# Attention values made token-major by transposing DMAs of 16-bit halves instead of float32 transposes on TensorE

## The chip, the cores and the metric

The kernel runs on one core of a Trainium2 chip. The metric is the device time of one execution in microseconds, as a median over runs; lower is better. The engines are named as the profile names them: PE is TensorE, DVE is VectorE, ACT is ScalarE, POOL is GpSimd, SP is SyncE, which issues most DMAs.

## The reference

Two layers work on 272 tokens (16 meta tokens and a sequence of 256) with 1024 features in float32. In each layer a mixer has three branches, and a convolutional feed-forward block follows:

```
proj = rms_norm(h) @ w_in          # rq rk rv rg  hq hf hi hg  dq dk dv  gates
o_ret = retention(rq, rk, rv, rg)  # 4 heads, values 256 wide
o_hg  = hgrn2(hq, hf, hi, hg)      # 8 heads, values 128 wide
o_da  = diff_attention(dq, dk, dv) # 8 heads, values 128 wide
y = sum(sigmoid(gates) * (branches @ w_branch))
h = h + y @ w_out
h = h + (silu(gate) * val) @ w_ffn_out   # gate, val: a convolution over tokens of rms_norm(h) @ w_ffn_in
```

The values of the three branches are rv, hi and dv. Each branch multiplies a matrix of weights between tokens by its values, so that the sum runs over tokens.

## The kernel before, in words

**Layout.** Features lie on the 128 partitions and tokens along the free dimension (T = 272). Each matrix product with a weight is three matmuls that take float32 apart into a rounded high part and a rest: `wh·xh`, `wh·xl`, `wl·xh` (L917 to L919, in `products`). One weight tile is 128 x 128, and one call of `products` makes two output tiles of 128 features (f = 0, 1), side by side in two PSUM banks (tag "main", two pairs of banks).

**Weights.** `_Weights` (L600) loads the weights in chunks of eight tiles, 128 x 1024 float32, by one DMA each on SP's queue (L628) into `wraw` (three buffers). ACT copies a chunk to `whi` (rounded), DVE subtracts to get `wlo`; both have four buffers. There are 404 chunks.

**Order.** The kernel does not issue instructions as its code runs. Each call through `_Engine` (L558) records an operation in `_Plan` with an engine, an assumed cost, a key (the time at which it is due), and the tiles that it reads and writes (`add`, L379, with overlaps found by `_span`, L370). `order` (L438) then simulates the five engines with these costs: an engine takes the operation that can start first, by key where several can, and `start` (L466) gives none before its buffers are free. What comes out is the fixed instruction order of every engine. The products have keys that follow each other on a clock; everything else is planned around them. `key += 2.0` moves what follows to a later due time. A sequence `ORDER` lists the products and, by marks, where the attention work of a branch begins to be spread between them and by when it has to be done.

**Values.** The matmuls of the attention need values with tokens on partitions, while `products` leaves features on partitions. `values` (L1491) lets ACT copy the two output tiles, 128 x 2 x 272, from PSUM to `vsrc` in SBUF (`evacuate`, L929). `to_tokens` (L953) then has PE transpose four blocks of 128 x 128 against an identity matrix into a PSUM bank (tag "bank", tile `vt`): two feature tiles by two blocks of 128 tokens. ACT copies the bank in two instructions of 128 x 256 to the token-major tile (`rvt`, or `vt` for hi and dv). The 16 tokens left over are gathered from `vsrc` by POOL into a tile `tails`, which `tail_tokens` (L962) transposes on PE once for each group of heads. In the loop over `ORDER` (L1555) the calls stand under `name == "rv"` (L1611) and `name in ("hi", "dv")` (L1620). rv, hi and dv have four calls each in a layer: 24 in all. In the order of work hi 0 and 1 come first, then hi 2, hi 3 and rv 0 to 3 in a row, then dv 0 and 1, and dv 2 and 3.

**Norms.** `mean` (L972) and `head_rsqrt` (L987) sum over partitions; both use a temporary tile "hso" for sums, and `head_rsqrt` lets POOL's all-reduce write it before ACT takes the logarithm and the exponential into `r`.

Of the kernel before, what the change touches and what calls it, by code (L numbers as in the profile page):

```python
# [11 lines left out]
F32 = mybir.dt.float32  # L12
F32R = mybir.dt.float32r
U8 = mybir.dt.uint8
AF = mybir.ActivationFunctionType
ALU = mybir.AluOpType
PSUM = bass.MemoryType.PSUM
# [2 lines left out]
P = 128  # L20
# [3 lines left out]
T = META + SEQ  # L24
# [13 lines left out]
TAIL = T - 2 * P  # L38
# [296 lines left out]
class _Plan:  # L335
# [34 lines left out]
    def _span(self, ap):  # L370
        step = ap.ap[0][0]
        lo = ap.offset % step
        hi = lo + 1 + sum((n - 1) * abs(s) for s, n in ap.ap[1:])
        if ap.tensor.name in self.psum:

            lo, hi = lo // BANK * BANK, -(-hi // BANK) * BANK
        return ap.tensor.name, lo, hi
# [60 lines left out]
    def order(self):  # L438

        times, mains = [m.key for m in self.main], set(self.main)  # L440
        for op in self.ops:
            i = bisect.bisect_right(times, op.key - EARLY) - 1
            if i >= 0 and op not in mains:
                self.queue(op, self.main[i])
        left = {}
        for op in self.ops:
            for n in op.tiles:
                left[n] = left.get(n, 0) + 1
        free = {tag: [0.0] * k for tag, k in self.room.items()}
        held, out = set(), []  # L450
        engines = {"pe": 0.0, "act": 0.0, "dve": 0.0, "pool": 0.0, "sp": 0.0}
        later = {e: [] for e in engines}
        now = {e: [] for e in engines}
        count = 0
        tables = "le"

        def push(op):
            nonlocal count
            count += 1
            heapq.heappush(later[op.engine], (op.ready, count, op))  # L460

        for op in self.ops:
            if op.need == 0:
                push(op)

        def start(op, t):  # L466

            want = {}
            for n in op.tiles:
                if n not in held:  # L470
                    want[self.tag[n]] = want.get(self.tag[n], 0) + 1
            for tag, k in want.items():
                if len(free[tag]) < k:
                    return None
                t = max(t, sorted(free[tag])[k - 1])
            return t

        def rank(op):
            late = 8.0 if op.func in self.SETS and self.SETS[op.func] != tables else 0.0
            return op.key + late  # L480

        self.end = engines
        self.busy = {e: 0.0 for e in engines}
        taken = 0.0

        def comes(op):
            return op.count < self.MANY or (int(taken) - self.BEGIN.start) % self.PIECE < len(self.BEGIN)

        todo = len(self.ops)
        while len(out) < todo:  # L490
            best = None
            for e, t0 in engines.items():
                while later[e] and later[e][0][0] <= t0:
                    _, c, op = heapq.heappop(later[e])
                    now[e].append((c, op))
                found = None
                for c, op in now[e]:
                    t = start(op, t0) if comes(op) else None
                    if t is not None and (found is None or (t, rank(op), c) < found[:3]):
                        found = (t, rank(op), c, op)  # L500
                if later[e]:
                    t1 = later[e][0][0]
                    if found is None or t1 < found[0]:
                        found = (t1, 0.0, -1, None)
                if found is not None and (best is None or found[0] < best[0]):
                    best = found + (e,)
            if best is None:
                raise RuntimeError("no order: " + str([(e, [o.tiles for _, o in now[e]][:4]) for e in now]))
            t, _, c, op, e = best
            if op is None:  # L510
                engines[e] = t
                continue
            now[e].remove((c, op))
            cost = op.cost
            if e == "dve" and engines["pool"] > t:

                cost += min(engines["pool"] - t, self.SHARED * cost)
            if op.func in self.SETS and self.SETS[op.func] != tables:
                tables = self.SETS[op.func]
                cost += self.SWITCH  # L520
                if tables == "le":
                    out.append(None)
                    todo += 1
            for n in op.tiles:
                if n not in held:
                    held.add(n)
                    f = free[self.tag[n]]
                    f.remove(min(f))
            engines[e] = t + cost
            self.busy[e] += cost  # L530
            taken += op.count * (1 + self.SEMS)
            done = t + cost + (2.0 if e == "sp" else 0.0)
            for n in op.tiles:
                left[n] -= 1
                if left[n] == 0:
                    free[self.tag[n]].append(done + self.FREE)
            for o in op.after:
                o.need -= 1
                o.ready = max(o.ready, done + (self.CROSS if o.engine != e else 0.0))
                if o.need == 0:  # L540
                    push(o)
            if op.run is not None:
                out.append(op)
            else:
                todo -= 1
        return out
# [11 lines left out]
class _Engine:  # L558
# [5 lines left out]
    def __getattr__(self, method):  # L564
        f = getattr(self.engine, method)

        def call(*args, **kw):
# [13 lines left out]
            if method == "reciprocal":  # L581
                cost += 7 * self.each * n
            elif method == "tensor_tensor_scan":
                cost += self.each * n
            elif method == "transpose":
                cost = 0.11
            elif method == "matmul" and args[1].dtype == F32R:
                cost = max(0.107, n / 2400 + 0.003)
            elif method == "matmul":
                cost = max(0.214 if args[1].shape[-1] > 32 else 0.07, 4 * n / 2400)  # L590
            elif method == "dma_start":
                cost = self.fixed + self.each * n * outs[0].shape[0]

# [60 lines left out]
def _trace(ctx, tc, plan, a, depth, probe):  # L654
# [35 lines left out]
    def temp(cols, tag, bufs=2):  # L690
        return new(tp, [P, cols], F32, tag, bufs, tag)
# [4 lines left out]
    def bank(name):  # L696
        return new(bp, [P, 512], F32, "bank", 2, name)
# [252 lines left out]
        act.activation(hi, x, AF.Copy)  # L950
        tt(lo, x, hi.bitcast(F32), SUB)

    def to_tokens(src, vt, e):  # L953

        pt = bank("vt").rearrange("p (f c e) -> p f c e", f=2, c=2)
        for f in range(2):
            for c in range(2):
                pe.transpose(pt[:, f, c, :], src[:, f, c * P : (c + 1) * P], ident)
        for f in range(2):
            act.activation(vt[:, :, e + f * P : e + (f + 1) * P], pt[:, f], AF.Copy)  # L960

    def tail_tokens(tails):  # L962

# [8 lines left out]
    def mean(ones_, x):  # L972
# [1 line left out]

        n = x.shape[1]
        sums = x[top]
        other = temp(T, "hso")[top, :n]
        act.activation(other, x[low], AF.Copy)
        tt(sums, sums, other, ADD)
        both = new(tp, [P, T], F32R, "hsh", 1, "hsh")[:, :n]  # L980
# [6 lines left out]
    def head_rsqrt(r, x, func, scale=1.0):  # L987

        n = x.shape[1]
        sq = x  # L990
        if func != AF.Copy:
            sq = temp(T, "hsq")[:, :n]
            act.activation(sq, x, func)
        sums = temp(T, "hso")[:, :n]
        pool.partition_all_reduce(sums, sq, channels=P, reduce_op=bass.bass_isa.ReduceOp.add)
        rsqrt(r, sums, scale / P)

    def split_blocks(name, blocks, t0):

# [8 lines left out]
    for li in range(depth):  # L1008
# [479 lines left out]
                st[name] = slot4(name)  # L1488
            return st[name]

        def values(ps, vt, e):  # L1491

            src = temp2("vsrc")
            evacuate(src, ps)
            plan.key += 2.0
            to_tokens(src, vt, e)
            return src

        def final():

            turns.pop(0)
# [53 lines left out]
        for name, j in ORDER:  # L1555
# [31 lines left out]
            if name in BASE:  # L1587
# [23 lines left out]
                elif name == "rv":  # L1611
                    if j == 0:
                        st["rvt"] = [slot("rvt")[:, : 8 * P].rearrange("p (c e) -> p c e", c=2) for _ in range(2)]
                        st["tails"] = temp(P, "tails")
                    src = values(ps, st["rvt"][j // 2], (j % 2) * 2 * P)
                    tails = st["tails"].rearrange("p (e h t) -> p e h t", e=2, h=4)
                    pool.tensor_copy(tails[:, :, j, :], src[:, :, 2 * P :])
                    if j == 3:
                        st["rvs"] = tail_tokens(st["tails"])
                elif name in ("hi", "dv"):  # L1620
                    n = name[0] + "v"
                    b = j // 2
                    if j % 2 == 0:
                        st[f"{n}t{b}"] = slot("vt")[:, : 8 * P].rearrange("p (c e) -> p c e", c=2)
                        st["tails"] = temp(P, "tails")
                        if name == "hi":
                            pool.memset(st["tails"][:, 4 * TAIL :], 0.0)
                    src = values(ps, st[f"{n}t{b}"], (j % 2) * 2 * P)
                    tails = st["tails"].rearrange("p (g h t) -> p g h t", g=2, h=4)[:, :, two, :]
                    pool.tensor_copy(tails[:, 0], src[:, :, 2 * P :])  # L1630
                    if name == "dv":
                        pool.tensor_copy(tails[:, 1], src[:, :, P : P + TAIL])
                    if j % 2:
                        st[f"{n}s{b}"] = tail_tokens(st["tails"])
                else:
# [101 lines left out]
```

## Time and profile before

| | |
|---|---|
| median of three runs | 1294.4 us (1294.36 to 1294.51) |
| the profiled execution's own time | 1293.94 us |
| its span in the profile | 1292.2 us |
| mean granted TensorE clock | 0.998 of full speed |
| HBM read | 216.19 MB, 168 GB/s over the span |

The span reaches from the first to the last instruction of the profiled execution. In the rows of the profile an instruction is named by line, engine, operation and tiles (out<-in), followed by counts, busy time and mean duration. All operations that the planner records have one line, L595 before the change, so groups are told apart by their tiles. "PEld" is the loading of weights into TensorE, which overlaps the matmuls; "SPq" is the instruction stream of SP, which issues DMAs. A row of waits reads: who waited, for whom, microseconds in total, times, longest.

### The profile page before, as it was taken

How to read it: one execution, taken by the hardware profiler on the slowest of the kernel's cores; microseconds unless marked ns; L12 is line 12 of the kernel's file. 1: busy time of each engine (PE TensorE's matmuls, PEld its weight loads, DVE VectorE, ACT ScalarE, POOL GpSimd, SP SyncE). 2: the span in 40 equal slices, each digit the busy share in tenths (PEclk: the TensorE clock that was granted, in tenths of full speed). 3: DMA queues.
4: the chain of work that ended last, by engine and by line, in shares of the span. 5: the costliest groups of instructions: out<-in, count | busy, mean ns of one | idle time of the engine just before them, and what ended most of it. 6: DMA issues, size and time to landing. Idle time of an engine off the chain costs nothing.

```text
span 1292.2 us, 27078 instructions
## 1 busy us (share of the span) xinstructions
PE 1284.3 (99%) x10921; PEld 1263.7 (98%) x10921; DVE 975.6 (75%) x1657; ACT 827.8 (64%) x1404; POOL 174.3 (13%) x206
## 2 busy tenths in 40 slices
PE   9999999999999999999999999999999999999998
PEld 9999999999999999999999999999999999999986
DVE  7685887698585789886565867976986867898753
ACT  6765465756576568776456664657566765787743
POOL 5001101313122020000020011012132220200000
PEclk9999999999999999999999999999999999999999
DMA  8644554444545555555555455544445466556653
GB/s 277 200 155 157 166 177 131 136 151 147 175 133 178 180 163 181 179 180 168 176 178 182 162 165 178 172 140 140 159 144 180 131 195 197 163 190 201 199 187 106
DMA packets 60750, 218.99 MB, mean 169 GB/s; under 512 B 6865, under 2 KB 6993, under 8 KB 60625
## 3 DMA queue, kind: packets, MB, share of 16 engines
q1 hardware_dynamic: 60336, 216.74, 52.1%
q8 instruction: 86, 1.41, 0.5%
q10 hardware_dynamic: 288, 0.52, 0.1%
q14 instruction: 40, 0.32, 0.1%
HBM read 216.19 MB, written 1.05 MB: 168 GB/s over the span
## 4 chain that ended last, share of the span: by engine, by line
PE 98%; DMA 0%; SPq 0%; DVE 0%; issue 0%; ACT 0%; DVEq 0%
PE main L919 29%; PE main L917 29%; PE main L918 28%; PE fo L1533 2%; PE fo L1531 2%; PE fo L1532 2%; PE ds L1394 1%; PE do L595 1%; PE ro L595 1%; PE ho L595 1%; PE vt L595 1%; PE lev L1117 1%; PE wt L595 1%; DMA wraw<-in_w 0%; PE s L595 0%; PE px L595 0%
## 5 line engine op out<-in xcount | busy, mean ns | idle before, releaser
L917 PE MATMUL main<-xh,whi 128*128 128x272 f32 (+1 forms) x2368 | 688.3, 291 | 0.5 <-ACT whi L595 0.5
L919 PE MATMUL main<-xh,wlo 128*128 128x272 f32 (+1 forms) x2368 | 679.4, 287 | 0.5 <-DVE wlo L595 0.4
L918 PE MATMUL main<-xl,whi 128*128 128x272 f32 (+1 forms) x2368 | 670.2, 283 | 0.0
L595 DVE TENSOR_TENSOR wlo<-wraw,whi 128x1024 fp32r<-128x1024 f32 (+1 forms) x408 | 509.4, 1254 | 200.5 <-ACT whi L595 197.2
L595 ACT ACTIVATE whi<-wraw 128x1024 fp32r<-128x1024 f32 (+1 forms) x408 | 426.6, 1048 | 221.3 <-PE main L918 143.9
L918 PEld LDWEIGHTS main<-xl,whi 128*128 128x128 f32 x2368 | 449.2, 190 | 0.4
L917 PEld LDWEIGHTS main<-xh,whi 128*128 128x128 f32 x2368 | 445.3, 188 | 1.9 <-ACT whi L595 0.7
L919 PEld LDWEIGHTS main<-xh,wlo 128*128 128x128 f32 x2368 | 444.5, 188 | 1.2 <-DVE wlo L595 1.1
L595 POOL PARTITION_ALL_REDUCE hso<-hsq x36 | 74.5, 2091 | 94.8 <-ACT hsq L595 94.6
L595 POOL TENSOR_TENSOR y<-h,rstd 128x272 f32<-128x272 f32 x32 | 37.9, 1215 | 319.5 <-ACT rstd L595 319.5
L595 DVE SCALAR_TENSOR_TENSOR two_b<-u,small,two_b 128x256 f32<-128x256 f32 (+2 forms) x176 | 78.4, 486 | 0.6 <-ACT two_b L595 0.2
L919 PE MATMUL main<-ghi,wlo 128*128 128x272 f32 x176 | 51.0, 290 | 0.0
L917 PE MATMUL main<-ghi,whi 128*128 128x272 f32 x176 | 50.8, 288 | 0.0
L918 PE MATMUL main<-glo,whi 128*128 128x272 f32 x176 | 50.1, 285 | 0.0
L595 ACT ACTIVATE two_b<-u,small 128x272 f32<-128x272 f32 (+1 forms) x88 | 49.3, 598 | 0.7 <-DVE glo L595 0.5
L595 ACT ACTIVATE u<-main 128x544 f32<-128x544 f32 (+1 forms) x40 | 24.5, 613 | 36.5 <-PE main L919 36.4
L595 POOL COPY tails<-vsrc 128x32 f32<-128x32 f32 x32 | 11.0, 360 | 209.2 <-ACT vsrc L595 203.0
L917 PE MATMUL main<-b0hi,whi 128*128 128x272 f32 (+1 forms) x128 | 37.7, 295 | 0.0
L917 PE MATMUL main<-b1hi,whi 128*128 128x272 f32 (+1 forms) x128 | 37.3, 292 | 0.0
L919 PE MATMUL main<-yhi,wlo 128*128 128x272 f32 (+1 forms) x128 | 36.5, 285 | 0.0
L919 PE MATMUL main<-b2hi,wlo 128*128 128x272 f32 (+1 forms) x128 | 36.5, 285 | 0.0
L919 PE MATMUL main<-b1hi,wlo 128*128 128x272 f32 (+1 forms) x128 | 36.5, 285 | 0.0
(264 smaller groups left out, 1946.8 us busy)
## 6 DMA issues: line engine op xcount, KB each, us to landing
wraw<-in_w SPq DMA_DIRECT2D x402, 512.0 KB, 3.5
h<-in_h SPq DMA_DIRECT2D x4, 272.0 KB, 5.1
dec<-in_dec SPq DMA_DIRECT2D x2, 544.0 KB, 4.4
wraw<-in_w SPq DMA_DIRECT2D x4, 256.0 KB, 4.7
const<-in_const SPq DMA_DIRECT2D x1, 937.0 KB, 7.6
gain<-in_gl SPq DMA_DIRECT2D x1, 512.0 KB, 4.4
out<-y ACTq DMA_DIRECT2D x2, 256.0 KB, 2.7
out<-y SPq DMA_DIRECT2D x2, 256.0 KB, 2.7
```

The source lines that it names most:

```text
L595: self.plan.add(self.name, lambda: f(*args, **kw), cost, outs, ins, args[2] if method == "activation" else None, count)
L917: nc.tensor.matmul(o, wh, hi, start=first, stop=False)
L918: nc.tensor.matmul(o, wh, lo, start=False, stop=False)
L919: nc.tensor.matmul(o, wl, hi, start=False, stop=last)
L1117: nc.tensor.matmul(o, keys, x, start=True, stop=True)
L1394: nc.tensor.matmul(ss[m][:, at : at + nk], q[half, hd, q0 : q0 + P], k[half, hd, :nk], start=True, stop=True)
L1531: nc.tensor.matmul(o, gh, wh, start=False, stop=False)
L1532: nc.tensor.matmul(o, gl, wh, start=False, stop=False)
L1533: nc.tensor.matmul(o, gh, wl, start=False, stop=end)
```

## The change

`to_tokens` takes the product's PSUM tiles. ACT reads their first 256 tokens as 16-bit words and writes all low halves, then all high halves, to a tile `vsrc` of 128 x 1024 words (two instructions of 128 x 512). One DMA on SP's queue, `dma_start_transpose`, transposes it in eight blocks of 128 x 128 words into `vtr`, which has one buffer. ACT joins the halves in two instructions of 128 x 512 words into the token-major float32 tile, which it writes as 16-bit words. `values` is gone; the tails are copied by ACT from PSUM, and not by POOL from `vsrc`. The branch for hi and dv changes in the same way as that for rv, with a second tail copy for dv. The planner learns the overlap of 16-bit tiles, a cost of 1.5 for the transposing DMA, and to hold buffers back for PE blocks of 200 or more instructions that are due earlier. The tile "hso" is given up: `mean` uses "hsq", and the all-reduce writes `r` itself.

```diff
@@ def _span @@
+        if ap.dtype == U16:
+            lo, hi = lo // 2, -(-hi // 2)
@@ def order: start @@
+            first = [o for _, o in now["pe"] if o.count >= self.MANY and o.key < op.key]
             for tag, k in want.items():
-                if len(free[tag]) < k:
+                if len(free[tag]) < k + sum(self.tag[n] == tag for o in first for n in o.tiles if n not in held):
                     return None
@@ class _Engine @@
+            elif method == "dma_start_transpose":
+                cost = 1.5
@@ def _trace @@
-    def to_tokens(src, vt, e):
-        pt = bank("vt").rearrange("p (f c e) -> p f c e", f=2, c=2)
-        for f in range(2):
-            for c in range(2):
-                pe.transpose(pt[:, f, c, :], src[:, f, c * P : (c + 1) * P], ident)
-        for f in range(2):
-            act.activation(vt[:, :, e + f * P : e + (f + 1) * P], pt[:, f], AF.Copy)
+    def half_words(t):
+        return t.bitcast(U16).rearrange("p a (t h) -> p h a t", h=2)
+
+    def to_tokens(ps, vt, e):
+        src = new(tp, [P, 2, 2, 2 * P], U16, "vsrc", 2, "vsrc")
+        words = half_words(ps[:, :, : 2 * P])
+        for h in range(2):
+            act.activation(src[:, h], words[:, h], AF.Copy)
+        plan.key += 1.0
+        turned = new(tp, [P, 8, P], U16, "vtr", 1, "vtr")
+        sync.dma_start_transpose(turned, src.rearrange("p h f t -> p (h f t)"))
+        plan.key += 4.0
+        turned = turned.rearrange("p (h f c) x -> p h c f x", h=2, f=2)
+        to = half_words(vt[:, :, e : e + 2 * P])
+        for h in range(2):
+            act.activation(to[:, h].rearrange("p c (f x) -> p c f x", f=2), turned[:, h], AF.Copy)
@@ def mean @@
-        other = temp(T, "hso")[top, :n]
+        other = temp(T, "hsq")[top, :n]
@@ def head_rsqrt @@
-        sums = temp(T, "hso")[:, :n]
-        pool.partition_all_reduce(sums, sq, channels=P, reduce_op=bass.bass_isa.ReduceOp.add)
-        rsqrt(r, sums, scale / P)
+        pool.partition_all_reduce(r, sq, channels=P, reduce_op=bass.bass_isa.ReduceOp.add)
+        rsqrt(r, r, scale / P)
-        def values(ps, vt, e):
-            src = temp2("vsrc")
-            evacuate(src, ps)
-            plan.key += 2.0
-            to_tokens(src, vt, e)
-            return src
@@ for name, j in ORDER: name == "rv" @@
-                    src = values(ps, st["rvt"][j // 2], (j % 2) * 2 * P)
-                    pool.tensor_copy(tails[:, :, j, :], src[:, :, 2 * P :])
+                    act.activation(tails[:, :, j, :], ps[:, :, 2 * P :], AF.Copy)
+                    to_tokens(ps, st["rvt"][j // 2], (j % 2) * 2 * P)
```

More of the change, by code (lines that the diff above doesn't have):

```diff
@@ L14 @@
 U8 = mybir.dt.uint8
+U16 = mybir.dt.uint16
 AF = mybir.ActivationFunctionType
@@ L1627, in _trace @@
                             pool.memset(st["tails"][:, 4 * TAIL :], 0.0)
-                    src = values(ps, st[f"{n}t{b}"], (j % 2) * 2 * P)
                     tails = st["tails"].rearrange("p (g h t) -> p g h t", g=2, h=4)[:, :, two, :]
-                    pool.tensor_copy(tails[:, 0], src[:, :, 2 * P :])
+                    act.activation(tails[:, 0], ps[:, :, 2 * P :], AF.Copy)
                     if name == "dv":
-                        pool.tensor_copy(tails[:, 1], src[:, :, P : P + TAIL])
+                        act.activation(tails[:, 1], ps[:, :, P : P + TAIL], AF.Copy)
+                    to_tokens(ps, st[f"{n}t{b}"], (j % 2) * 2 * P)
                     if j % 2:
```

## The prediction

> **What bounds the kernel now.** I read the busy shares first, then the chain that ended last, then the waits of TensorE alone.
>
> ```profile
> span 1292.2 us, 27078 instructions
> PE 1284.3 (99%) x10921; PEld 1263.7 (98%) x10921; DVE 975.6 (75%) x1657; ACT 827.8 (64%) x1404; POOL 174.3 (13%) x206
> PE 98%; DMA 0%; SPq 0%; DVE 0%; issue 0%; ACT 0%; DVEq 0%
> ```
>
> TensorE has 99% of the span, and 98% of the chain is TensorE after TensorE. A busy PE need not be PE at its peak, so the waits decide. In the view of what each engine waited for, TensorE's whole list is this:
>
> ```profile
> PE warm L595 <- POOL ones_d L595: 1.0, 1, 1.0
> PE main L917 <- ACT whi L595: 0.5, 1, 0.5
> PE main L919 <- DVE wlo L595: 0.4, 2, 0.2
> ```
>
> That is 1.9 us in the span. TensorE is an unbroken stream: an instruction taken out of it shortens the kernel by its step in the stream, as long as nothing else comes late.
>
> **What is removed.** One group of four transposes, in order of time on TensorE:
>
> ```profile
> 74.85 0.29 PE L917 MATMUL main<-xh,whi 128*128 128x272 f32 x1
> 74.98 0.28 PE L918 MATMUL main<-xl,whi 128*128 128x272 f32 x1
> 75.10 0.29 PE L919 MATMUL main<-xh,wlo 128*128 128x272 f32 x1
> 75.23 0.60 PE L595 MATMUL vt<-const,vsrc 128*128 128x128 f32 x4
> 75.59 0.37 PE L917 MATMUL main<-xh,whi 128*128 128x272 f32 x1
> 75.80 0.28 PE L918 MATMUL main<-xl,whi 128*128 128x272 f32 x1
> ```
>
> Durations overlap (0.29 us each, but a start every 0.125 us), so a step in the stream is read from starts. From 75.10 to 75.80 there are 0.70 us; two products alone would take 2 x 0.125 = 0.25. The four transposes cost 0.45 us, 0.11 us each.
>
> ```profile
> L595 PE MATMUL vt<-const,vsrc x96: 270/272/331, 75.2 to 978.7; 128*128 128x128 f32 x96
> L595 POOL COPY tails<-vsrc x32: 204/212/1067, 74.6 to 977.9; 128x32 f32<-128x32 f32 x32
> L595 ACT ACTIVATE vsrc<-main x24: 623/626/630, 73.9 to 976.5; 128x544 f32<-128x544 f32 x24
> L595 ACT ACTIVATE vt<-vt x32: 366/384/395, 75.9 to 979.5; 128x256 f32<-128x256 f32 x32
> L595 ACT ACTIVATE rvt<-vt x16: 362/379/392, 169.6 to 839.4; 128x256 f32<-128x256 f32 x16
> ```
>
> 96 transposes are 24 groups, 12 in each layer: 24 x 0.45 = 10.8 us; I take 10.7, since a few groups stand next to a tail transpose, which stays. (Summing the 272 ns durations would give 26 us; that is the mistake to avoid.) The order of the changed program's TensorE instructions has these 96 fewer and nothing else added or removed.
>
> The Trainium skill (VectorE: DVE Perf Modes, The three transpose paths) gives a TensorE transpose 390 ns in bf16. Here one costs 0.11 us of the stream, so a gain by the page, 96 x 0.39 = 37 us as an estimate from it, is not to be had.
>
> **What is added on ScalarE.** Per group: 32 tail columns straight from PSUM (before on GpSimd), two partings of 512 halves from PSUM, two joinings of 512 halves from SBUF. No row has 16-bit operands; the nearest by size and source:
>
> ```profile
> L595 ACT ACTIVATE sq<-fo 128x512 f32<-128x512 f32 x4 | 2.4, 598 | 6.9 <-PE fo L1533 6.9
> L595 ACT ACTIVATE extra<-hq 128x512 f32<-128x512 f32 x4 | 2.7, 668 | 0.0
> L595 ACT ACTIVATE qt<-hq 128x32 f32<-128x32 f32 x12 | 2.7, 224 | 0.0
> ```
>
> A group takes 2 x 0.60 + 2 x 0.67 + 0.22 = 2.76 us, in place of 0.63 + 2 x 0.38 = 1.39: 1.37 us more, 33 us in the kernel. The bounds: half the time, if 16-bit elements went two at a time, and twice, about 1.2 us each, if every half word cost a full word's access. I take the f32 rows: the copies have as many elements and the same four-byte steps.
>
> ScalarE is 64% busy, but what counts is the densest stage. In the stretch with six groups in a row (hi 2 and 3, rv 0 to 3):
>
> ```profile
> core 0: us, PE busy (x) PEld busy (x) DVE busy (x) ACT busy (x) POOL busy (x), PEclk, DMA share, GB/s
> 153.00:193.00 40.00, 40.00 (x381) 39.76 (x380) 31.35 (x62) 26.83 (x55) 4.90 (x10) 1.00 0.54 177
> 800.00:842.00 42.00, 42.00 (x524) 41.56 (x523) 34.57 (x74) 27.64 (x59) 5.90 (x12) 1.00 0.54 176
> ```
>
> 26.8 + 6 x 1.37 = 35.0 us of ScalarE in a stretch that shrinks to 40 - 6 x 0.45 = 37.3. It fits, with 2.3 us over. I allow 1 us in all for these two stretches (0 to 3).
>
> **What is added on the DMA queue.** 24 transposing transfers of 128 x 1024 x 2 B = 256 KB on SP's queue, between the weight loads. The trace has none; the rows to bound one:
>
> ```profile
> q1 hardware_dynamic: 60336, 216.74, 52.1%
> wraw<-in_w SPq DMA_DIRECT2D x402, 512.0 KB, 3.5
> out<-y SPq DMA_DIRECT2D x2, 256.0 KB, 2.7
> const<-in_const SPq DMA_DIRECT2D x1, 937.0 KB, 7.6
> ```
>
> By bytes: q1 moved 216.74 MB in 0.521 x 1292 = 673 us of the 16 engines, 322 GB/s; 256 KB take 0.8 us. A load (1.6 us by bytes) lands after 3.5, so 1.9 are fixed, and 0.8 + 1.9 = 2.7 is just what the 256 KB row shows. By packets: one took 673 x 16 / 60336 = 0.18 us of an engine for 3.6 KB; if each 256 B row of a block cost as much, 1024 rows over 16 engines would take 11.4 us, landing after 13. So 2.7 to 13 us. I take 4: the 256 KB row, plus part of a 1.6 us load that may stand ahead in the queue.
>
> The Trainium skill (DMA: Bandwidth & Descriptors, Latency and other measured facts) has transposing DMAs at 261 GB/s effective; 256 KB would then move in about 1.0 us, an estimate from that page, close to the lower end.
>
> What hides the landing? The joining waits for it on ScalarE, in order, and behind the joining stand the next weight splits (whi), partings and gates. The changed order puts between a group's last parting and its first joining 3 to 15 ScalarE instructions. With the durations of before they add up to 2.4 to 8.3 us, on average 5.4 over the 24 (the shortest has two whi of 1.05 and a tail copy). A landing at 4 us is late in three of the groups, by 0.6 to 1.6 us. What covers that:
>
> ```profile
> L595 ACT ACTIVATE whi<-wraw 128x1024 fp32r<-128x1024 f32 (+1 forms) x408 | 426.6, 1048 | 221.3 <-PE main L918 143.9
> ACT whi L595 <- PE main L918: 143.9, 112, 5.1
> ACT whi L595 <- DMA wraw<-in_w: 30.2, 25, 3.6
> SPq L595 <- DVE wlo L595: 809.0, 298, 8.3
> ```
>
> The first two rows: a split takes 1.05 us, and 112 times ScalarE waited for TensorE to free a split buffer, so splits run ahead, up to three chunks of 8 x 3 x 0.124 = 3.0 us. The last row: SP nearly always stands at a load that waits for a free buffer. A transfer that waits for a parting holds the loads behind it, but these are three buffers ahead; I cost that at nothing, and if the cover is gone it shows as ScalarE waiting for wraw, which cost TensorE nothing in the third row's 25 times.
>
> The rest: the all-reduce in place and the shared hsq buffer only lengthen two buffers' lives on GpSimd, 13% busy: 0, at most 1 us either way. The planner's new condition holds PSUM tiles for blocks of 200 or more instructions: 0, at most 2 us. A main PSUM pair is read for 1.4 us instead of 0.6, of the 5.9 us until its turn comes again: 0.
>
> **Sum.** The profiled execution took 1293.94 us, 1.7 outside its span. 1293.9 - 10.7 + 1.0 = 1284.2; the median of the three runs stands 0.5 above the profiled one: **1284.5 us**.
>
> **Rivals.**
>
> Late landing (the other side). If transfers land at 7 us, between the 512 KB row and the 937 KB row's 7.6, the average gap of 5.4 is short by 1.6, 24 x 1.6 = 38 us of ScalarE; ScalarE's spare time and the chunks ahead take perhaps a third of it, 25 stay: 1294.4 - 10.7 + 25 = 1309. It decides from about 6 us on, where 24 x 0.6 = 14 uses up gain and spare. For it: a queue shared with loads at a 0.54 share. Against: the 2.7 of the 256 KB row.
>
> Paid per row of 256 B. At 13 us every group is late by 7.6: 182 us, less 10.7: about 1460. For it: nothing in the trace has short rows in number. The Trainium skill (VectorE: DVE Perf Modes, The three transpose paths and its rules) points this way: 1309 ns for a 128x128 bf16 block through the DMA crossbar, so eight blocks that do not overlap would take 10.5 us, an estimate from that page, and it says to use TensorE where PSUM can take the result; no run here shows it yet.
>
> ScalarE becomes the bound. At 1.2 us for each 16-bit copy a group takes 5.0 us, 3.6 more: 26.8 + 21.7 = 48.5 in 37.3 us; 11 us over, less some 3 to 6 of chunks ahead, in two layers 10 to 16, and a few at the pairs: 1294 - 10.7 + 18 = 1302.
>
> No gain because the steps close up otherwise (the stream limited by loads): 1294. Against it: TensorE's own list of waits, 1.9 us in all.
>
> **How the numbers follow.** Forecast 1284.5, own range 1282 to 1289: 0.64. Landings at 5 to 6 us that eat most of the gain, or no gain, 1291 to 1297: 0.06. Late landing: 0.17. ScalarE: 0.06. Per row: 0.07. A measurement can tell about 0.2% from no change, 2.6 us. Faster 0.64, same 0.06, slower 0.30. Range: low 1282, which the removed steps allow with nothing lost; high 1315, which holds the late landing up to 7.3 us and ScalarE, and leaves out the per-row case and the later landings, under 2 in 10.
>
> **What would show it.** Right: no vt<-const,vsrc, TensorE's wait list still near 2 us, span near 1283; the new transfer lands within 5 us; partings near 0.60 and joinings near 0.67; ScalarE's waits for vtr few. Wrong: ScalarE waiting for the vtr transfer by more than 30 us in all, then TensorE waiting for whi, or for a main pair not yet parted, in the stretches around 153 to 193 and 800 to 842; or 16-bit copies near 1.2 us, with the same waits but no late transfer.

## The result, and the profile after

| | before | changed |
|---|---|---|
| median of four runs | 1294.38 us (1294.22 to 1294.51) | 1285.63 us (1284.91 to 1286.2) |
| ratio to before | | 0.9932, 95% interval 0.9915 to 0.9949 |
| profiled execution, its span | 1293.94, 1292.2 us | 1286.2, 1284.4 us |

The changed kernel is 8.7 us faster. The profiled execution happens to be the slowest of the four runs of the changed kernel, so its span shows 7.8 us.

The page of the changed kernel, the same lines as before, and the DMA queue (packets, MB, share of 16 engines):

```profile
span 1284.4 us, 26932 instructions
PE 1275.5 (99%) x10825; PEld 1253.6 (98%) x10825; DVE 973.0 (76%) x1657; ACT 855.6 (67%) x1460; POOL 165.9 (13%) x174
...
q1 hardware_dynamic: 85680, 223.03, 56.9%
...
PE 98%; DVE 1%; ACT 1%; DMA 0%; issue 0%; SPq 0%
```

TensorE has 96 instructions fewer and is still 98% of the chain; ScalarE has 27.8 us more. The queue has 25344 packets more, 1056 for each of the 24 transfers. 1% of the chain has gone over to VectorE and 1% to ScalarE. The new tile `vtr` in the trace (min/median/max in ns; the last line is the landing of the transfer):

```profile
L601 ACT ACTIVATE vt<-vtr x32: 752/778/809, 80.5 to 978.2; 128x512 uint16<-128x512 uint16 x32
L601 SPq DMA_TRANSPOSE vtr<-vsrc x24: 1237/1238/1879, 75.4 to 972.7; - x24
L601 ACT ACTIVATE rvt<-vtr x16: 764/786/807, 172.9 to 835.6; 128x512 uint16<-128x512 uint16 x16
...
  DMA vtr<-vsrc: 0.7, 1
...
DMA to landing us min/median/max: 3.0/3.6/5.3
```

A transfer lands 3.6 us after its issue, in the median; a joining takes 0.78 us. In 24 groups ScalarE waited once for a transfer, 0.7 us. The partings, from the view of the tile `vsrc`:

```profile
L601 ACT ACTIVATE vsrc<-main x48: 572/598/617, 74.3 to 972.0; 128x512 uint16<-128x512 uint16 x48
```

What TensorE waited for, all of it:

```profile
PE warm L601 <- POOL ones_d L601: 1.0, 1, 1.0
PE ro L601 <- DVE wts L601: 0.5, 1, 0.5
PE px L601 <- DVE near L601: 0.5, 1, 0.5
PE main L925 <- DVE wlo L601: 0.4, 2, 0.2
PE ro L601 <- DVE at L601: 0.3, 1, 0.3
PE main L923 <- ACT whi L601: 0.2, 1, 0.2
```

The waits at ro and px are new, and each delays the products behind it by more than its own row. In order of time:

```profile
849.07 0.28 PE L924 MATMUL main<-xl,whi 128*128 128x258 f32 x1
849.19 0.28 PE L925 MATMUL main<-xh,wlo 128*128 128x258 f32 x1
849.93 0.70 PE L601 MATMUL ro<-wts,rvt 128*128 128x258 f32 x2 [0.46 <-DVE wts L601]
```

From one start to the next are 0.74 us where 0.12 is usual. There are four such steps over 0.335 us after the start-up (at 210, 751, 752 and 849 us); together they are 1.9 us longer than a usual step, and the kernel before has none.

The stretch with six groups, in the changed kernel:

```profile
153.00:193.00 40.00, 40.00 (x377) 39.76 (x377) 32.55 (x64) 31.70 (x65) 2.46 (x4) 1.00 0.77 196
```

ScalarE went from 26.8 to 31.7 us there, and the DMA share from 0.54 to 0.77.

### The profile page after: what moved, and what is told of

It is laid out like the page before. It is cut to its first block, busy times and chain, and to the rows that moved or that the text cites. A ratio compares the mean times of both kernels' runs of the same rounds, so it can differ in the third digit from the quotient of the medians.

```text
span 1284.4 us, 26932 instructions
## 1 busy us (share of the span) xinstructions
PE 1275.5 (99%) x10825; PEld 1253.6 (98%) x10825; DVE 973.0 (76%) x1657; ACT 855.6 (67%) x1460; POOL 165.9 (13%) x174
## 4 chain that ended last, share of the span: by engine, by line
PE 98%; DVE 1%; ACT 1%; DMA 0%; issue 0%; SPq 0%
PE main L925 29%; PE main L923 29%; PE main L924 28%; PE fo L1538 2%; PE fo L1540 2%; PE fo L1539 2%; PE ds L1409 1%; PE ro L601 1%; PE do L601 1%; PE ho L601 1%; PE lev L1132 1%; PE wt L601 0%; PE s L601 0%; DMA h<-in_h 0%; PE far L1132 0%; PE px L601 0%
## 5 line engine op out<-in xcount | busy, mean ns | idle before, releaser
L601 POOL PARTITION_ALL_REDUCE hr<-hsq x36 | 75.5, 2119 | 147.6 <-ACT hsq L601 147.5
L923 PE MATMUL main<-b1hi,whi 128*128 128x272 f32 (+1 forms) x128 | 37.3, 292 | 0.0
L925 PE MATMUL main<-b0hi,wlo 128*128 128x272 f32 (+1 forms) x128 | 36.5, 285 | 0.0
```

The source lines that it names most:

```text
L601: self.plan.add(self.name, lambda: f(*args, **kw), cost, outs, ins, args[2] if method == "activation" else None, count)
L923: nc.tensor.matmul(o, wh, hi, start=first, stop=False)
L925: nc.tensor.matmul(o, wl, hi, start=False, stop=last)
```

## The experiments

The kernel before ran beside each group of experiments, at 1294.0 to 1294.3 us. Each ratio is to that.

### A transpose twice: its price

```diff
-                pe.transpose(pt[:, f, c, :], src[:, f, c * P : (c + 1) * P], ident)
+                for _ in range(2):
+                    pe.transpose(pt[:, f, c, :], src[:, f, c * P : (c + 1) * P], ident)
```

> The kernel before with each of the 96 value transposes issued twice in a row on TensorE into the same place. Theory (a transpose costs its step in the stream, 0.11 us): 96 x 0.11 = 10.7 us more, 1305.1, between 1304 and 1307. Rival (a transpose costs its duration of 0.27 us, or the 390 ns that the Trainium skill's page VectorE: DVE Perf Modes gives): 1320 to 1332.

1304.99 us, ratio 1.0087 (1.0072 to 1.0102): 11.0 us more for 96 transposes, 0.114 us each. The group of eight in order of time:

```profile
74.99 0.29 PE L919 MATMUL main<-xh,wlo 128*128 128x272 f32 x1
75.12 1.03 PE L595 MATMUL vt<-const,vsrc 128*128 128x128 f32 x8
75.92 0.37 PE L917 MATMUL main<-xh,whi 128*128 128x272 f32 x1
76.12 0.29 PE L918 MATMUL main<-xl,whi 128*128 128x272 f32 x1
```

From 74.99 to 76.12 are 1.13 us, less 0.25 for the products: 0.88 for eight, 0.11 each. The step in the stream is the price, and the duration of 0.27 us is not. The 390 ns of the Trainium skill (VectorE: DVE Perf Modes, The three transpose paths) are not the price here either.

### The side edits alone

```diff
+            first = [o for _, o in now["pe"] if o.count >= self.MANY and o.key < op.key]
...
-        other = temp(T, "hso")[top, :n]
+        other = temp(T, "hsq")[top, :n]
...
-        pool.partition_all_reduce(sums, sq, channels=P, reduce_op=bass.bass_isa.ReduceOp.add)
+        pool.partition_all_reduce(r, sq, channels=P, reduce_op=bass.bass_isa.ReduceOp.add)
```

> The kernel before with the side edits alone: the tile hso given up, the all-reduce in place, the planner's new condition for PE blocks of 200 or more instructions; the transposes stay on TensorE. Theory (the gain is the 96 transposes that leave TensorE's stream, 10.7 us, less about 2 us of new waits that come with the re-planned order): within 1.5 us of 1294.4. Rival (the side edits make part of the gain, or of the 2 us): 1292 or less, or 1296 or more.

1294.57 us, ratio 1.0003 (0.9995 to 1.0012). They neither gain nor lose, and none of the new waits is there. The gain is the transposes'.

### The transfer late by 3.4 us

```diff
-        sync.dma_start_transpose(turned, src.rearrange("p h f t -> p (h f t)"))
+        flat = src.rearrange("p h f t -> p (h f t)")
+        def twice(turned=turned):
+            nc.sync.dma_start_transpose(turned, flat)
+            nc.sync.dma_start_transpose(turned, flat)
+        plan.add("sp", twice, 1.5, [turned], [flat])
```

> The changed kernel with each of the 24 transposing transfers issued twice in a row into the same tile, the second after the first has landed; the planner is not told, so the order of every engine is that of the changed kernel. The pair should land some 7 us after the first issue, where one took 3.6. Theory of the prediction (5.4 us of ScalarE's work lie between parting and joining, and beyond that each microsecond costs up to 24 us): 1.6 to 2 us over, 1300 to 1325, with ScalarE waiting for vtr 30 us or more. Rival (the splits made ahead hide a far later landing): 1285 to 1290, with ScalarE's waits for vtr but none of TensorE.

1324.19 us, ratio 1.0243 (1.0226 to 1.026): 38.4 over the changed kernel's 1285.77 when it was run again. From the first issue to the second landing are 7.0 us on average over the 24 (6.1 to 9.2). ScalarE's and TensorE's waits in this kernel:

```profile
ACT vt L601 <- DMA vtr<-vsrc: 34.6, 16, 3.6
...
ACT rvt L601 <- DMA vtr<-vsrc: 25.7, 8, 5.4
```

```profile
PE px L601 <- DVE am L601: 4.4, 1, 4.4
PE lev L1138 <- DVE extra L601: 3.9, 1, 3.9
PE wt L601 <- DVE wts L601: 3.4, 2, 1.9
PE lev L1138 <- ACT extra L601: 3.4, 1, 3.4
PE vm L601 <- ACT tails L601: 3.0, 3, 1.6
PE far L1138 <- DVE hq L601: 3.0, 1, 3.0
```

ScalarE waited in all 24 groups, 60.3 us. The profiled span is 37.4 us over the changed kernel's. TensorE's steps over 0.335 us are 31.1 us longer than usual in all, against 1.9 in the changed kernel. It does not wait for split weights: its list has 0.2 us for whi and 0.6 us for wlo. It waits for the attention's own chain (px, lev, wt, far), which runs over ScalarE and VectorE behind the joining. One such chain, picked from the views of the three engines in order of time:

```profile
178.92 1.40 ACT L601 ACTIVATE rvt<-vtr 128x512 uint16<-128x512 uint16 x2 [2.27 <-DMA vtr<-vsrc]
181.12 0.88 ACT L601 ACTIVATE extra<-hq 128x816 f32<-128x816 f32 x1
183.10 0.44 DVE L601 TENSOR_TENSOR extra<-extra,tot 128x272 f32<-128x272 f32 x1
183.68 1.94 PE L1138 MATMUL lev<-extra,hf 128*32 128x64 f32 x64 [3.87 <-DVE extra L601]
```

ScalarE stands idle for 2.27 us before the joining, its copy to `extra` stands behind it, VectorE's steps on `extra` behind that, and TensorE's `lev` waits for the last of them. Most of the other 8 us are a slower step of the products: without those over 0.335 us it is 124.3 ns on average in place of 123.8 over some 9030 of them, 5 us in all. They have a place, as the granted clock (the number before the DMA share) shows:

```profile
160.00:180.00 20.00, 19.51 (x155) 19.07 (x153) 12.23 (x25) 12.04 (x24) 0.00 (x0) 1.00 0.75 188
180.00:200.00 20.00, 14.71 (x151) 14.38 (x152) 14.88 (x31) 14.47 (x33) 0.00 (x0) 0.83 0.69 195
182.70:189.50 6.80, 5.82 (x81) 5.68 (x82) 6.54 (x15) 3.84 (x11) 0.00 (x0) 0.50 0.68 204
836.00:860.00 24.00, 20.63 (x210) 20.11 (x212) 15.83 (x31) 14.94 (x32) 0.00 (x0) 0.86 0.76 188
```

Where TensorE waited for several microseconds, its granted clock fell to 0.83 and 0.86 on average over a stretch; in every fortieth of the changed kernel's span it is 0.9 or more. In the trace's own record the clock stands at 0.50 in four places before the kernel's end, 20 us together (one of them is the third row). Each begins 3 to 5 us after the start of one of the four steps that are longer than 3 us (3.2, 3.7, 4.2 and 4.7 us). Behind the next longest step, of 2.8 us, there is none. The Trainium skill (TensorE: Matmul & The Clock Gate, Why this matters for your kernels) warns of pauses over some 3 us between bursts of matmuls; the trace agrees, with its four steps of 3.2 to 4.7 us.

### A small transfer ahead of each

```diff
-        sync.dma_start_transpose(turned, src.rearrange("p h f t -> p (h f t)"))
+        flat = src.rearrange("p h f t -> p (h f t)")
+        spare = new(tp, [P, 2, P], U16, "vspare", 1, "vspare")
+        def twice(turned=turned):
+            nc.sync.dma_start_transpose(spare, flat[:, : 2 * P])
+            nc.sync.dma_start_transpose(turned, flat)
+        plan.add("sp", twice, 1.5, [turned, spare], [flat])
```

> The changed kernel with a small transposing transfer (two blocks into a spare tile) issued on SP's queue just before each of the 24; the planner is not told, and the engines' orders stay. It holds SP for about 1.2 us, so the values' transfer should land about 4.8 us after it could have been issued, instead of 3.6. Theory (on average 5.4 us of ScalarE's work hide it, and the splits made ahead the few groups that have less): 1285 to 1288. Rival (each microsecond of landing costs from the start, as the step from 3.6 to 7.0 us may have cost 11 us for each): 1296 to 1300.

1285.45 us, ratio 0.9933 (0.9918 to 0.9948), like the changed kernel. From the first issue to the landing of the values are 5.2 us on average (4.3 to 6.5). The row of the small transfer, and all that ScalarE waited for at the joinings:

```profile
L975 SPq DMA_TRANSPOSE vspare<-vsrc x24: 1173/1175/2171, 74.4 to 970.9; - x24
...
  DMA vtr<-vsrc: 4.1, 4
```

The values are not late by 1.5 us, though. The small transfer reads only what the first parting wrote, and it goes out 0.44 us before the second parting ends, on average. Counted from that end the values land after 4.8 us on average, where they land after 4.25 in the changed kernel and after 8.4 (6.1 to 14.9) in the kernel with each transfer twice. At the rival's 11 us for each microsecond of landing these 0.55 us would have cost 6 us.

So a landing 4.8 us behind the parting costs nothing that can be measured, and one 8.4 us behind it costs 38 us. The knee lies between, and so do the 5.4 us of ScalarE's work in the prediction; these runs do not place it more closely.

### Where the last two microseconds are

Five kernels ask why TensorE now waits 1.9 us. ScalarE with one joining of 1024 in place of two of 512 (the partings write their blocks in another order for it, which is left out here):

```diff
...
-        for h in range(2):
-            act.activation(to[:, h].rearrange("p c (f x) -> p c f x", f=2), turned[:, h], AF.Copy)
+        act.activation(to, turned, AF.Copy)
```

> The changed kernel with the two joinings of 512 half words made one of 1024 (the partings write another order of blocks so that the joining is a plain three-dimensional copy). If a joining's 0.78 us has some 0.2 us of fixed cost, a group saves 0.2 us of ScalarE, 5 us in all. Theory (the 2 us that TensorE now waits come from where the new order puts VectorE's steps ahead of a ro or px product, not from ScalarE's load): 1284 to 1287, no clear change. Rival (ScalarE's load is what makes TensorE wait): 1283.5 to 1284.5, and TensorE's waits for wts and near gone.

1285.92 us, ratio 0.9938 (0.9925 to 0.995). A joining of 1024 takes 1.38 us, 0.18 less than two of 512 by their durations. But two in a row overlap, and ScalarE's busy time falls by 1.6 us only (854.0 in place of 855.6). Nothing follows from it in the time, and as a test of ScalarE's load it is a weak one.

ScalarE with half of the joining left out:

```diff
+        pool.memset(vt[:, :, e : e + 2 * P], 0.0)
-        for h in range(2):
-            act.activation(to[:, h].rearrange("p c (f x) -> p c f x", f=2), turned[:, h], AF.Copy)
+        act.activation(to[:, 1].rearrange("p c (f x) -> p c f x", f=2), turned[:, 1], AF.Copy)
```

> The changed kernel without the joining of the low halves (the values keep their high 16 bits; GpSimd zeroes the tile instead), so 24 x 0.78 = 19 us less of ScalarE; the planner plans for it. Theory (the waits of TensorE that are left, 1.9 us, come from where the new order places VectorE's steps before ro and px products): no clear change, 1284 to 1287, with TensorE waiting for VectorE still at one or more ro or px products. Rival (ScalarE's load makes them): 1283 to 1284, and those waits gone.

1284.69 us, ratio 0.9928 (0.9915 to 0.994). Of the new waits one is left (ro for wts, 0.2 us). The median is 0.9 us under the changed kernel's, but the intervals overlap; 15 us less of ScalarE (840.9 busy in place of 855.6) bought at most that.

The planner told the new costs, the joining due later, and the planner told the pace of TensorE and VectorE:

```diff
+                if ins[0].dtype == U16 and ins[0].tensor.name not in self.plan.psum:
+                    cost += 0.21
...
-                cost = 1.5
+                cost = 1.25
```

> The changed kernel with the planner told what the profile shows of the new steps: 0.21 more for a joining, 1.25 instead of 1.5 for the transfer's hold of SP. Theory (the 1.9 us come of the order as a whole, not of these costs): 1283.5 to 1287, with the waits at other places or the same. Rival (the wrong costs of the new steps cause the waits): 1283 to 1284, waits gone.

```diff
-        plan.key += 4.0
+        plan.key += 6.0
```

> The changed kernel with the joining due 6.0 instead of 4.0 after the transfer. Theory (a landing at 3.6 is hidden already, and any change of keys deals the order anew): no clear change, 1283.5 to 1287, ScalarE's wait for vtr 1 us or less as before. Rival (joinings too early in ScalarE's order cost time): 1 to 2 us faster than the changed kernel.

```diff
-    dve = _Engine(plan, nc.vector, "dve", 0.068, 1.042e-3)
+    dve = _Engine(plan, nc.vector, "dve", 0.072, 1.10e-3)
...
-        cost = 3 * ((T - t0) / 2400 + 0.003)
+        cost = 3 * ((T - t0) / 2400 + 0.0105)
```

> The changed kernel with the planner told the measured pace of TensorE's products (0.124 us each instead of 0.116) and of VectorE (costs 5% up). Theory (the leftover waits come of an order planned with VectorE's steps too short): TensorE's waits for VectorE after the start go from 1.9 us to under 0.5, and 1283.5 to 1285. Rival (the leftover is chance of the order, or of ScalarE): 1285 to 1290, with waits at other places.

They took 1285.26 (0.993, 0.9917 to 0.9942), 1286.17 (0.994, 0.9927 to 0.9954) and 1287.56 us (0.995, 0.9938 to 0.9962). The theory that a planner with truer speeds would remove the waits fell: the last one is 1.9 us slower than the changed kernel, and TensorE waits at other places, for wlo, am, ho:

```profile
PE main L925 <- DVE wlo L601: 1.4, 3, 1.0
PE warm L601 <- POOL ones_d L601: 1.0, 1, 1.0
PE main L923 <- ACT whi L601: 0.6, 1, 0.6
PE ro L601 <- DVE am L601: 0.4, 1, 0.4
```

In the kernel with the joining due later, the profiled execution is the fastest of the five: 1284.68 us, with one new wait of 0.3 us at ro. The other four took 1286.01 to 1287.04 us with the same order of instructions. So executions of one order differ by as much as the waits in question.

One kernel more has the single joining and its measured cost together:

```diff
+        act.activation(to, turned, AF.Copy)
...
+                if ins[0].dtype == U16 and ins[0].tensor.name not in self.plan.psum:
+                    cost += 0.34
```

> The changed kernel with one joining of 1024 half words instead of two of 512, and with the planner told its measured 1.38 us and the transfer's 1.25. Theory (the small waits left are chance of the order): 1283.5 to 1286.5, not clearly different from the changed kernel. Rival (ScalarE's load and wrong costs make them): 1283 to 1284.3.

1286.03 us, ratio 0.9937 (0.9925 to 0.995). And the changed kernel again:

> The changed kernel once more, beside the others of this call: 1284.9 to 1286.3, 8 to 9.5 us under the kernel before.

1285.77 us, ratio 0.9934 (0.9922 to 0.9946). Its profiled execution waits at px 0.7 and at ro 0.8, and once for whi 1.1.

### What makes a joining slower than a parting

```diff
-        to = half_words(vt[:, :, e : e + 2 * P])
+        to = vt[:, :, e : e + 2 * P].bitcast(U16).rearrange("p a (h t) -> p h a t", h=2)
...
-            act.activation(to[:, h].rearrange("p c (f x) -> p c f x", f=2), turned[:, h], AF.Copy)
+            act.activation(to[:, h].rearrange("p c (f x) -> p c f x", f=2), turned[:, 1], AF.Copy)
```

> The changed kernel with joinings that write their half words one behind the other instead of into every second one (both joinings copy the high halves, so the values are scrambled and the low halves left out). If writing with a four-byte step is what makes a joining take 0.78 us instead of the 0.60 of a parting: 0.60 to 0.67 here. If not (reading 16-bit words from SBUF costs it): 0.78 as before. The time of the kernel stays within 1.5 us of 1285.6 either way.

The one run took 1285.29 us, and the joinings are these:

```profile
L601 ACT ACTIVATE vt<-vtr x32: 609/620/652, 79.7 to 976.9; 128x512 uint16<-128x512 uint16 x32
L601 ACT ACTIVATE rvt<-vtr x16: 614/636/642, 172.1 to 834.3; 128x512 uint16<-128x512 uint16 x16
```

Writing half words into every second place costs 0.16 us of the 0.78. Reading words with that step, as the partings do from PSUM, costs nothing next to the f32 rows of the kernel before (0.598 and 0.598).

## Why the prediction was right, point by point

- **The bound.** Right. TensorE's stream set the time, and it still does.
- **The removed 10.7 us.** Right, and shown from the other side: doubling the transposes cost 11.0 us. That it was read from starts and not from durations decided it; by durations it would have been 26 us.
- **ScalarE.** The partings at 0.60 are as costed, the joinings 0.78 in place of 0.67. Busy time rose by 27.8 us in place of 33, because instructions in a row overlap (two partings take 1.08 us together); the durations by themselves add up to 40 us more. In the dense stretch 31.7 us of 40 are used, where I had 35.0 of 37.3. It is not the bound: taking 15 us off it moved the time by 0.9 at most.
- **The landing.** I took 4 us out of 2.7 to 13; it is 3.6. The bound by packets (11.4 us) was far too high. In the trace's DMA records the 24576 packets of 256 B took 0.026 us of one engine on average, 1.7 us of the 16 engines for each transfer. The queue's share rose by more, from 673 us (0.521 x 1292.2) to 731 us (0.569 x 1284.4), 2.4 us for each transfer; the rest is the loads, whose packets of 4 KB went from 0.203 to 0.208 us. The trace of the kernel before could have told: its packets of 4 KB took 0.203 us, those of 2 KB 0.097 and a few of 128 B 0.014. The rival that each short row costs as much as a long one is refuted. With it falls the estimate of 10.5 us from the 1309 ns that the Trainium skill (VectorE: DVE Perf Modes, The three transpose paths) gives for a block. The estimate of 1.0 us from the 261 GB/s of the Trainium skill (DMA: Bandwidth & Descriptors, Latency and other measured facts) is under these 1.7 us, if the packets' time is read as work.
- **What hides it.** Right in its place: no loss when the values land 4.8 us behind the parting, a loss at 8.4. The working counted the landing as if the issue followed the parting at once; it follows after 0.56 us on average, and up to 2.4. Of the three groups that were to be late, one was, by 0.7 us.
- **The price of a late landing.** Wrong in size. I had 1309 for 7 us, from 24 x 1.6 = 38 us of ScalarE, a third of it taken by ScalarE's spare time and by chunks ahead; with a landing 7.0 us after the first issue ScalarE waited 60.3 us, and the kernel took 1324.2. The splits ahead covered TensorE's products as expected, but not its attention matmuls, which stand in the same order of instructions and wait for a chain behind the joining; and the granted clock fell after these waits, some 5 us more. Had the rival come true, my range's end at 1315 would have been too low.
- **The allowance of 1 us.** The term was too small and stood for the wrong thing. 1.9 us are lost, not in the dense stretches to ScalarE but at single ro and px products that wait for VectorE. That puts the profiled execution at 1293.9 - 10.7 + 1.9 = 1285.1, of 1286.2 measured; about 1 us of it I cannot place. Measured against the forecast, the median is 1.1 us higher. That it is no more is in part luck: the same work in other orders took 1285.3 to 1287.6 us.
- **Planner, buffers and the loads held back, at nothing.** Right for the edits by themselves (1.0003). Right for the loads: ScalarE's waits for `wraw` rose from 30.2 to 43.0 us, but TensorE waited for `whi` 0.2 us in all. What I left out is that every re-planned order has its own small waits.

What stays open is which of the planner's choices puts VectorE's steps late before these products. Less work on ScalarE, truer costs and other due times gave 1284.7 to 1287.6 us, with waits at changing places; only the kernel with all paces changed stands apart, its five runs (1287.46 to 1287.9) above every run of the changed kernel. No version is shown to beat the changed kernel.

## What to carry to other kernels

Where one engine is an unbroken stream, price an instruction by the distance between starts, and then ask of the work that replaces it only whether it lands before the waiting engine gets there: here 5.4 us of other instructions stood between the parting and the joining, a landing 4.8 us behind the parting cost nothing, and one 8.4 us behind it cost 38. A late result on an engine that works in order delays everything behind it, so splits made ahead do not protect the matmuls that hang on the same chain.

## What the runs showed of the hardware

- SP is held 1.24 us by each transposing transfer of 128 x 1024 words, and by 1.17 us by one of two blocks (the row of the spare tile), so it is hardly the size that holds it.
- ScalarE copies 512 words of 16 bits in the time of 512 float32 (0.598 us from PSUM); written with a four-byte step they take 0.78 instead of 0.62 us.
- With each transfer issued twice, the granted clock fell to 0.50 behind each of TensorE's four steps of 3.2 to 4.7 us, for 3.4 or 6.8 us, and not behind one of 2.8 us.
- A 256 B packet of a transposing transfer took 0.026 us of a DMA engine on average, a 4 KB packet of a load 0.208.
